# Feed-forward of a Hymba layer on Trainium2: SyncE's transfers in program order, token sums stored eight sums behind, block loads and row stores at steps of their own

## The chip, the cores and the metric

The kernel runs on one core of a Trainium2 chip. The metric is the device time of one execution in microseconds (us). Its runs took 2438.16, 2438.87 and 2443.68 us, a median of 2438.87 us. The execution that the profiler recorded took 2437.08 us, of which 2435.3 us is the span of its trace; 1.8 us lie outside the span. Where a time of the trace is named, it counts from the start of that span.

## The reference

The layer has 2048 tokens of width 1024: two mixers (gated linear attention and dilated sliding-window attention), an output projection, and a feed-forward part with a hidden width of 4096 and a squared ReLU. All of it is computed in float32. The change lies in the feed-forward part alone:

```
h = h + matmul(square(relu(matmul(rmsnorm(h, mlp_norm_g), W_ff1))), W_ff2)
y = rmsnorm(h, final_norm_g)
```

W_ff1 is 1024 x 4096 and W_ff2 is 4096 x 1024.

## The kernel before, in words

Every float32 operand of a matmul is split into a rounded part and the rest of it (`split`: ScalarE writes the rounded part at L414, VectorE the rest at L415), and `mm3` makes three matmuls of 128 x 128 by 128 x 512 of each pair (L134, L135, L136). So each operand passes ScalarE and VectorE before TensorE can use it.

**First matmul of the feed-forward part (FF1 below, 1127 to 1828 us).** The work is cut into 32 blocks g: two halves of the tokens by 16 slices of 256 hidden columns. A block is done in 7 jobs instead of 8, by a scheme of Strassen's kind, in the order 1, 2, 5, 6, 3, 4, 7; a job is 12 matmuls. `prep1` makes the weight operand of a job two jobs ahead: it splits a piece of the block's raw weights, and between the jobs VectorE adds and subtracts pieces of them in place (L1158 after job 1's and 2's split, L1160 to L1163 later). There are two raw buffers, `w1raw`, so the load of block g+2 (`load_w1`, L1143, 1 MB) may be issued only once the split for job 7 of block g is done, and L1158 of block g+2 waits for it. `product1` runs the 12 matmuls and takes the bank out of PSUM; the results of a block are four tiles c11, c12, c21, c22 in `acc1`, to which ScalarE applies ReLU and the square (L1186, L1187). c21 and c22 come last, with job 7 (VectorE L1201 to L1203 ahead of them).

**Token sums.** The second matmul works on sums of hidden blocks. After every two blocks, 14 jobs, `token_sums` is begun: 28 additions on GpSimd (`SUMS`, L1224), on pieces of 128 x 256 in the `acc1` tiles and in three scratch pieces at the end of the tile `xt`. Each entry of `SUMS` is (result, left, sign, right, index of the stored result or None); 0 to 15 are pieces of the two blocks, 16 and above the scratch. SyncE writes 26 results of a pair of blocks to the array `actD` in device memory (L1218): four pieces as they are (`SINGLES`) and those sums that have an index. One pair of blocks is called a period below.

**Second matmul (FF2 below, 1828 us to the end).** 26 products of two halves make 52 phases of 48 matmuls. A phase is 8 steps of 6 matmuls; steps are counted from the start of FF2, and FF1's last jobs have negative steps, two to a job. `load_s` reads a token operand from `actD` into the buffers `rs` (L1282), `prep_s` splits it into `cs` (L1296, L1298, L1300); `load_t` reads a block of weights into `rt` or, for the third buffer, into two `acc1` tiles (L1312); `add_t` adds or subtracts weight blocks on GpSimd (L1320) and stores one result as `tD`; `prep_t` splits into `ct`. `load_c` reads rows of h into `sum` or `acc1` (L1336), `taken` adds the phase's banks to them, and `output` normalizes the rows and stores them (L1355, L1356). Functions are run at the steps given by the tables at the end.

**What sets the order.** On every engine instructions run in the order in which the scheduler of the language has put them. It works from the program's order and its own estimate of durations and may move an instruction ahead of others. SyncE (SP in the profile, SPq for its queue) only issues transfers: one that waits holds up all that stand behind it.

Of the kernel before, what the change touches and what calls it, by code (L numbers as in the profile page):

```python
# [69 lines left out]
SUMS = [  # L70
# [7 lines left out]
]  # L78
# [27 lines left out]
NB = 6  # L106


def emit(tc, a, stop=99):
# [38 lines left out]
    xt = const.tile([128, 1280], F32, name="xt")  # L148
# [1058 lines left out]
    def act_tiles(g):  # L1207

        t = [acc1[(g - g % 2 + k // 2) % 4][:, 1024 * (k % 2) + 256 * m:1024 * (k % 2) + 256 * m + 256]
             for m in range(4) for k in range(4)]  # L1210
        return t + [xt[:, 512 + 256 * i:768 + 256 * i] for i in range(3)]

    def token_sums(g):

        half, c, t = g // NP, g % NP // 2, act_tiles(g)

        def store(r, v):
            SP.dma_start(actD[r, half, :, c], v)  # L1218

        for l, r in SINGLES:  # L1220
            store(r, t[l])
        yield
        for l, x, op, y, r in SUMS:
            G.tensor_tensor(t[l], t[x], t[y], op=OP.add if op == "+" else OP.subtract)  # L1224
            if r is not None:
                store(r, t[l])
            yield
# [56 lines left out]
    def prep_s(ph, u):  # L1284
# [16 lines left out]
        load_s(ph + 2, u)  # L1301
# [12 lines left out]
    def add_t(q, u):  # L1314

        _, _, _, add, stored = WEIGHTS[q]
        if add is not None:
            d, x, op, y = add
            d, x, y = [traw(b, u // 2)[:, u % 2 * 2:u % 2 * 2 + 2] for b in (d, x, y)]
            G.tensor_tensor(d, x, y, op=OP.add if op == "+" else OP.subtract)  # L1320
            if stored:
                SP.dma_start(tD[:, 2 * u:2 * u + 2], d)
# [15 lines left out]
    def output(half, l, i):  # L1338
# [16 lines left out]
        SP.dma_start(out2[row:row + 128, 512:], C[1])  # L1355
        (A if (half, l, i) == (1, 3, 1) else SP).dma_start(out2[row:row + 128, :512], C[0])  # L1356
# [18 lines left out]
    steps = {}  # L1375
# [4 lines left out]
    def step(n):  # L1380
        for f, args in steps.pop(n, ()):
            f(*args)

    for ph in range(2 * NR):
        for u, n in ((0, -7), (1, -3)):
            at_step(4 if (ph, u) == (1, 1) else 8 * ph + n, prep_s, ph, u)
    for q, at in enumerate(first_of):
        at *= 16
        for h, n in ((0, -23), (1, -17)):
# [12 lines left out]
    rb.append(slot("rb"))  # L1402
    back = [*back, reload(order[3], 0), reload(order[4], 0), reload(order[5], 0, slot("rt"))]
    load_w1(1)
    for at in range(7):
        if at == 2:
            norm_to_T(*late)
        if back:
            list(back.pop(0))
        if at == 1:  # L1410
            back.append(reload(order[6], 0))
        prep1(at + 2)
        product1(at)


    first, parts_at = 7 * (NP - 1), {}
    for n in range(14):
        parts_at.setdefault(first + 1 + n * 4 // 5, []).append(n // 2)
    halves, begun = {}, set()
    ts = iter(())  # L1420
    for at in range(7, len(jobs1)):
        if at == first - 2:
            halves.update({n: reload(order[n], 1) for n in range(2)})
        prep1(at + 2)
        product1(at)
        for _ in range(2 if at % 14 else 3):
            next(ts, None)
        if at % 14 == 13:
            ts = token_sums(at // 7)
        for n in parts_at.get(at, ()):  # L1430
            next(halves[n])
            if n in begun and n + 2 < 7:
                halves[n + 2] = reload(order[n + 2], 1)
            begun.add(n)
        for n in range(2):
            step(2 * (at - len(jobs1)) + n)

    P, left = {}, None
    for ph in range(2 * NR):
        if PRODUCTS[ph // 2][1]:  # L1440
            P[ph % 2] = [bank() for _ in range(2)]
        p = P[ph % 2]
        for k in range(8):
            step(8 * ph + k)
            if ph == 0:
                for _ in range(3 if k < 4 else 5):
                    next(ts, None)
            if left and k < 2:
                taken(ph - 1, k, left[k])
            if ph < 2 * NR - 1 or k < 2:  # L1450
                for i in range(2):
                    mm2(p[i], ph, k, i)
        left = p
    for i in range(2):
        for k in range(2, 8):
            mm2(left[i], 2 * NR - 1, k, i)
        taken(2 * NR - 1, i, left[i])
# [55 lines left out]
```

## Time and profile before

| what | value |
|---|---|
| runs, median of 3 | 2438.87 us |
| profiled execution, its own time | 2437.08 us |
| its span | 2435.3 us |
| PE busy | 2292.4 us, 94% of the span |
| DVE busy | 1704.7 us, 70% |
| POOL busy | 1179.3 us, 48% |
| ACT busy | 1166.5 us, 48% |
| mean granted TensorE clock | 0.976 |
| transfers | 430.78 MB, mean 177 GB/s |

PE is TensorE's matmuls, DVE VectorE, ACT ScalarE, POOL GpSimd. An engine's share is a mean over stages that have different limits, so a stage is read from its own rows: how many matmuls it ran, how long they took, and what PE waited for. In a row of waits the columns are the waiting engine, its tile and line, the engine or transfer that released it, and then us in total, how often, and the longest. In a row of the timeline stand the start, the length, engine, line, operation, result and inputs, and in brackets the idle time of the engine before it with what ended it. One execution was recorded; its time stands 1.8 us below the median of the runs.

### The profile page before, as it was taken

Reading aid. Unit: us, or ns where it says so; the run is one execution under the profiler, and the core shown is the slowest. Engines: PE = TensorE matmul, PEld = TensorE weight load, DVE = VectorE, ACT = ScalarE, POOL = GpSimd, SP = SyncE. Lnnn points to the kernel's source line nnn. Section 1 sums busy time; section 2 is a strip of 40 time slices with the busy share of each in tenths; the row PEclk is TensorE's granted clock in tenths of the full one; section 3 lists DMA queues with packets and bytes.
Section 4 is the critical chain, followed back from the end, with each engine's and each line's share of the span. In section 5 each row is a group of like instructions: output and inputs, shape, how many; then the busy total and the mean of one; then the engine's idle time right before and its main releaser. Section 6 shows DMA issues by size and latency. Waiting matters only on the chain. (4 is left out here: it accounts for less than half of the span.)

```text
span 2435.3 us, 35693 instructions
## 1 busy us (share of the span) xinstructions
PE 2292.4 (94%) x12456; PEld 1964.1 (81%) x12456; DVE 1704.7 (70%) x2802; ACT 1166.5 (48%) x2227; POOL 1179.3 (48%) x1098
## 2 busy tenths in 40 slices
PE   6999999999999998999998898899899899999998
PEld 6877998789999996888777776777677688888877
DVE  6888768766667774457666568666676787866896
ACT  5565436435777771234444446444443333333454
POOL 5333324345478684000466466666564752431674
PEclk8999999999999999999999899999999999999999
DMA  6458744767667773677343447443348653534463
GB/s 155 120 167 244 246 148 125 239 191 236 193 215 226 248 245 114 206 258 254 117 128 119 126 132 222 139 130 120 122 128 288 206 200 127 193 119 142 140 233 117
DMA packets 340371, 430.78 MB, mean 177 GB/s; under 512 B 20773, under 2 KB 270134, under 8 KB 333663
## 3 DMA queue, kind: packets, MB, share of 16 engines
q1 hardware_dynamic: 340046, 428.24, 55.4%
q8 instruction: 98, 1.61, 0.3%
q14 instruction: 83, 0.67, 0.1%
q10 hardware_dynamic: 144, 0.26, 0.0%
HBM read 276.60 MB, written 156.54 MB: 178 GB/s over the span
## 5 line engine op out<-in xcount | busy, mean ns | idle before, releaser
L415 DVE TENSOR_TENSOR w1comb<-w1raw,w1comb 128x512 fp32r<-128x512 f32 x224 | 186.9, 838 | 65.3 <-ACT w1comb L414 65.1
L414 ACT ACTIVATE w1comb<-w1raw 128x512 fp32r<-128x512 f32 x224 | 135.5, 624 | 200.8 <-DVE w1raw L1160 179.3
L1296 ACT ACTIVATE cs<-rs 128x1024 fp32r<-128x1024 f32 x104 | 109.2, 1051 | 190.1 <-PE ps_c L136 92.9
L724 ACT ACTIVATE pe<-pe,O 128x256 f32<-128x256 f32 (+1 forms) x384 | 155.8, 454 | 57.8 <-DVE O L723 53.2
L752 PE MATMUL ps_a<-v,pt 128*128 128x65 f32 x1200 | 179.6, 251 | 0.7 <-DVE pt L742 0.7
L752 PEld LDWEIGHTS ps_a<-v,pt 128*128 128x128 f32 x1200 | 175.6, 194 | 2.2 <-DVE pt L742 0.9
L1224 POOL TENSOR_TENSOR xt<-acc,acc 128x256 f32<-128x256 f32 x48 | 45.0, 937 | 259.9 <-ACT acc L1187 207.7
L162 POOL TENSOR_TENSOR stats<-stats,mhalf 128x1 f32<-128x1 f32 (+1 forms) x64 | 46.1, 723 | 247.4 <-DVE stats L161 247.3
L733 PE MATMUL ps_d<-ident,pe 128*128 128x128 f32 x600 | 159.9, 279 | 0.0
L723 DVE CUSTOM_DVE_ANT_0 pe<-ps_c,nb 128x256 f32<-128x256 f32 (+1 forms) x384 | 126.8, 361 | 42.0 <-PE ps_d L733 17.6
L415 DVE TENSOR_TENSOR ct<-rt,ct 128x1024 fp32r<-128x1024 f32 x68 | 121.6, 1794 | 41.2 <-ACT ct L414 41.1
L135 PE MATMUL ps_c<-hb,w1comb 128*128 128x512 f32 x336 | 134.9, 401 | 16.3 <-DVE w1comb L415 16.3
L1186 ACT ACTIVATE acc<-acc 128x512 f32<-128x512 f32 x128 | 80.4, 631 | 142.7 <-DVE acc L1198 59.7
L270 ACT ACTIVATE wcomb<-wraw 128x512 fp32r<-128x512 f32 (+2 forms) x126 | 96.6, 773 | 96.6 <-POOL wraw L276 20.0
L136 PE MATMUL ps_c<-ct,cs 128*128 128x512 f32 x360 | 141.9, 394 | 0.0
L134 PE MATMUL ps_c<-ct,cs 128*128 128x512 f32 x360 | 141.8, 394 | 0.0
L135 PE MATMUL ps_c<-ct,cs 128*128 128x512 f32 x360 | 141.6, 393 | 0.0
L1224 POOL TENSOR_TENSOR acc<-acc,acc 128x256 f32<-128x256 f32 x128 | 139.5, 1094 | 2.4
L134 PE MATMUL ps_c<-hb,w1comb 128*128 128x512 f32 x336 | 133.5, 397 | 1.0 <-ACT w1comb L414 1.0
L1158 DVE TENSOR_TENSOR w1raw<-w1raw 128x512 f32<-128x512 f32 x32 | 22.4, 701 | 159.1 <-DMA w1raw<-w_ff 159.1
L136 PE MATMUL ps_c<-hb,w1comb 128*128 128x512 f32 x336 | 133.1, 396 | 0.0
L1224 POOL TENSOR_TENSOR acc<-acc 128x256 f32<-128x256 f32 x128 | 128.1, 1006 | 3.8
(370 smaller groups left out, 7960.3 us busy)
## 6 DMA issues: line engine op xcount, KB each, us to landing
rs<-actD SPq DMA_DIRECT2D x103, 512.0 KB, 4.6
actD<-acc SPq DMA_DIRECT2D x304, 128.0 KB, 2.0
w1raw<-w_ff SPq DMA_DIRECT2D x32, 1024.0 KB, 6.7
rt<-w_ff SPq DMA_DIRECT2D x24, 1024.0 KB, 6.4
k<-kD SPq DMA_DIRECT2D x16, 1024.0 KB, 8.3
actD<-xt SPq DMA_DIRECT2D x112, 128.0 KB, 1.9
rb<-hTD SPq DMA_DIRECT2D x13, 1024.0 KB, 6.8
wraw<-w_in SPq DMA_DIRECT2D x48, 256.0 KB, 3.6
```

What stands on the lines that cost most here:

```text
L134: T.matmul(out, sh, mh, start=first, stop=False, skip_group_check=more)
L135: T.matmul(out, sl, mh, start=False, stop=False, skip_group_check=more)
L136: T.matmul(out, sh, ml, start=False, stop=last, skip_group_check=more)
L270: A.activation(hi, src, AF.Copy, scale=sc)
L414: A.activation(hi, src, AF.Copy)
L415: V.tensor_tensor(lo, src, hi.bitcast(F32), op=OP.subtract)
L723: V.tensor_tensor_reduce(p, s, bias, scale=1.0, scalar=BIG, op0=OP.add, op1=OP.min, accum_out=nm)
L724: A.activation(p, p, AF.Exp, bias=nm, scale=-1.0)
L733: T.transpose(pb[:, i * 128:i * 128 + 128], src, ident)
L752: T.matmul(self.b.opsum[:, n % 4], self.pt[:, i * 128:i * 128 + 128], self.b.v[:, blk, cols], start=first, stop=last)
L1224: G.tensor_tensor(t[l], t[x], t[y], op=OP.add if op == "+" else OP.subtract)
L1296: A.activation(v[:, 0, cs], x, AF.Copy, scale=float(sign))
```

## The change

SyncE's instructions of the feed-forward part are taken out of the scheduler's hands (`tc.manual_schedule(engines={SP.engine})`): they are issued in the order in which the program writes them. The other engines are scheduled as before. Beside it:

- `SUMS` is a new list of 28 sums that gives the same stored results, with four scratch pieces: two in `xt`, two in the upper half of `gM`. `xt` is 256 elements shorter.
- The store of a sum is written `BEHIND` = 8 sums after it, the stores of `SINGLES` at the third sum. Three sums are written after each job (two before, three after the first job of a period), and those of the last period over the phases 0 to 3 (all in phase 0 before).
- `load_s` leaves `prep_s` and is written at steps of its own, 15 steps ahead of the `prep_s` that uses it; the first `load_t` of a weight block and the first `prep_s` of a phase are one step later.
- Stores of `tD` and of output rows are written 4 steps later, but for those of the last 6 steps.

The body of the feed-forward part is only indented; what else changes in it is shown.

```diff
-    xt = const.tile([128, 1280], F32, name="xt")
+    xt = const.tile([128, 1024], F32, name="xt")
...
-        return t + [xt[:, 512 + 256 * i:768 + 256 * i] for i in range(3)]
+        return t + [v[:, 512 + 256 * i:768 + 256 * i] for v in (xt, gM) for i in range(2)]
...
-        for l, r in SINGLES:
-            store(r, t[l])
-        yield
-        for l, x, op, y, r in SUMS:
-            G.tensor_tensor(t[l], t[x], t[y], op=OP.add if op == "+" else OP.subtract)
-            if r is not None:
-                store(r, t[l])
+        for i in range(len(SUMS) + BEHIND):
+            if i == 2:
+                for l, r in SINGLES:
+                    store(r, t[l])
+            if i >= BEHIND and SUMS[i - BEHIND][4] is not None:
+                store(SUMS[i - BEHIND][4], t[SUMS[i - BEHIND][0]])
+            if i < len(SUMS):
+                l, x, op, y, _ = SUMS[i]
+                G.tensor_tensor(t[l], t[x], t[y], op=OP.add if op == "+" else OP.subtract)
             yield
...
-        load_s(ph + 2, u)
...
-                SP.dma_start(tD[:, 2 * u:2 * u + 2], d)
+                at_step(now[0] + 4, SP.dma_start, tD[:, 2 * u:2 * u + 2], d)
...
-        SP.dma_start(out2[row:row + 128, 512:], C[1])
-        (A if (half, l, i) == (1, 3, 1) else SP).dma_start(out2[row:row + 128, :512], C[0])
+        later(out2[row:row + 128, 512:], C[1])
+        if (half, l, i) == (1, 3, 1):
+            A.dma_start(out2[row:row + 128, :512], C[0])
+        else:
+            later(out2[row:row + 128, :512], C[0])
...
+    def later(*args):
+
+        if now[0] < 16 * NR - 6:
+            at_step(now[0] + 4, SP.dma_start, *args)
+        else:
+            SP.dma_start(*args)
...
-        for u, n in ((0, -7), (1, -3)):
+        for u, n in ((0, -6), (1, -3)):
             at_step(4 if (ph, u) == (1, 1) else 8 * ph + n, prep_s, ph, u)
+            if ph > 1:
+                at_step(max(8 * ph + n - 15, 9 if (ph, u) == (3, 1) else -99), load_s, ph, u)
...
-        for h, n in ((0, -23), (1, -17)):
+        for h, n in ((0, -22), (1, -17)):
...
+    with tc.manual_schedule(engines={SP.engine}):
...
-        for _ in range(2 if at % 14 else 3):
+            for _ in range(3):
...
-            if ph == 0:
-                for _ in range(3 if k < 4 else 5):
+                if ph < 4:
+                    for _ in range(2 - k % 2):
```

The first place is SyncE's queue in a middle period of FF1. Before, this stands ahead of and behind the load of an odd block (`w1raw_11505`); `actD_102<-` is a store of a token sum, "waits Pool_49" a wait for the sum itself, "DMAHW" one for an earlier transfer:

```order
776 L1218 DMA actD_102<-acc1_11520 128x256 [waits DMAHW0_49,Pool_49]
777 L1218 DMA actD_102<-acc1_11520 128x256 [waits DMAHW1_49,Pool_49]
778 L1218 DMA actD_102<-acc1_11520 128x256 [waits DMAHW2_49,Pool_49]
779 L1218 DMA actD_102<-acc1_11520 128x256 [waits DMAHW3_49,Pool_49]
780 L1218 DMA actD_102<-acc1_11519 128x256 [waits DMAHW4_49,Pool_49]
781 L1218 DMA actD_102<-acc1_11520 128x256 [waits DMAHW5_49,Pool_49]
782 L1218 DMA actD_102<-xt_74 128x256 [waits DMAHW6_49,Pool_49]
783 L1143 DMA w1raw_11505<-w_ff1 128x8x256 [waits DMAHW7_49,DVE_49]
784 L1218 DMA actD_102<-acc1_11517 128x256 [waits DMAHW0_49,Pool_49]
```

In the changed kernel the same place on SyncE, with the load of an odd block as `w1raw_11507`:

```order
793 L1219 DMA actD_102<-acc1_11520 128x256 [waits DMAHW1_49,Pool_49]
794 L1219 DMA actD_102<-acc1_11520 128x256 [waits DMAHW2_49,Pool_49]
795 L1219 DMA actD_102<-acc1_11519 128x256 [waits DMAHW3_49]
796 L1219 DMA actD_102<-acc1_11519 128x256 [waits DMAHW4_49]
797 L1219 DMA actD_102<-gs_10008 128x256 [waits DMAHW5_49]
798 L1219 DMA actD_102<-acc1_11519 128x256 [waits DMAHW6_49]
799 L1219 DMA actD_102<-xt_74 128x256 [waits DMAHW7_49]
800 L1219 DMA actD_102<-gs_10008 128x256 [waits DMAHW0_49]
801 L1219 DMA actD_102<-acc1_11519 128x256 [waits DMAHW1_49,Pool_49]
802 L1219 DMA actD_102<-acc1_11520 128x256 [waits DMAHW2_49]
803 L1144 DMA w1raw_11507<-w_ff1 128x8x256 [waits DMAHW3_49,DVE_49]
```

Before, each store ahead of the load waits for its own sum, and the last one, from `xt`, stores a sum of the next period. Now row 794 stores the sum that GpSimd makes as the 27th of the period's 28, row 801 waits for the 28th, and the others in between were made before these; three stores of the period stand behind the load.

The second place is GpSimd at the begin of the last period, which runs into FF2. Before (`xt_74` is the scratch, the `acc1` tiles are the two blocks):

```order
886 L1224 TENSOR_TENSOR xt_74<-acc1_11519,acc1_11520 128x256 [waits Activation_49]
887 L1224 TENSOR_TENSOR acc1_11519<-acc1_11520 128x256 [waits Pool_49]
888 L1224 TENSOR_TENSOR acc1_11520<-acc1_11520 128x256 [waits DMAHW0_49,Pool_49]
889 L1224 TENSOR_TENSOR xt_74<-acc1_11520 128x256 [waits DMAHW6_49]
890 L1224 TENSOR_TENSOR xt_74<-acc1_11519,xt_74 128x256 [waits DMAHW4_49,Pool_49]
```

The same place in the changed kernel (`gs_10008` holds the two new scratch pieces, the blocks' tiles have other numbers):

```order
885 L1229 TENSOR_TENSOR xt_74<-acc1_11521,acc1_11522 128x256 [waits DMAHW6_49,Activation_49]
886 L1229 TENSOR_TENSOR gs_10008<-acc1_11521,xt_74 128x256 [waits DMAHW1_49,Pool_49]
887 L1229 TENSOR_TENSOR acc1_11522<-acc1_11521,acc1_11522 128x256
888 L1229 TENSOR_TENSOR acc1_11522<-acc1_11522 128x256
889 L1229 TENSOR_TENSOR acc1_11521<-acc1_11521 128x256 [waits Pool_49]
890 L1229 TENSOR_TENSOR gs_10008<-gs_10008 128x256 [waits Pool_49]
891 L1229 TENSOR_TENSOR acc1_11521<-acc1_11521 128x256 [waits Pool_49]
892 L1229 TENSOR_TENSOR acc1_11521<-acc1_11522,acc1_11521 128x256 [waits Pool_49]
893 L1229 TENSOR_TENSOR acc1_11522<-acc1_11522 128x256 [waits DMAHW3_49]
```

Before, row 889 overwrites a scratch piece that an early sum of the same period left there to be stored, so it waits for that store; now the pieces written in the first rows are those of the period before, and the first piece that is overwritten behind a store of the same period comes at row 893.

The third place is ScalarE where FF2 begins. Before (`ct` is a weight operand made of the raw weights `rt`, `cs` a token operand made of `rs`, or of `acc1` for the last piece of phase 1):

```order
1579 L1187 ACTIVATE acc1_11520<-acc1_11520 128x512 [waits Activation_49] x2
1580 L414 ACTIVATE ct_16599<-rt_16502 128x1024 [waits DMAHW1_49,PE_49]
1581 L1296 ACTIVATE cs_16449<-rs_16306 128x768 [waits DMAHW2_49,PE_49]
1582 L414 ACTIVATE ct_16661<-rt_16502 128x1024
1583 L1296 ACTIVATE cs_16449<-acc1_11520 128x256 [waits PE_49,Activation_49]
```

The same place in the changed kernel:

```order
1576 L1188 ACTIVATE acc1_11522<-acc1_11522 128x512 [waits Activation_49] x2
1577 L1299 ACTIVATE cs_16483<-rs_16311 128x768 [waits DMAHW5_49,PE_49]
1578 L1299 ACTIVATE cs_16483<-acc1_11522 128x256 [waits PE_49,Activation_49]
1579 L415 ACTIVATE ct_16587<-rt_16508 128x1024 [waits DMAHW6_49]
1580 L415 ACTIVATE ct_16627<-rt_16508 128x1024
```

The two pieces of the token operand of phase 1 stood behind the weight operand `ct`; now they stand ahead of it. VectorE's instructions for the same tiles are moved in the same way. In the rest of FF1, VectorE, ScalarE and TensorE keep their order.

More of the change, by code (lines that the diff above doesn't have):

```diff
@@ L106 @@
 NB = 6
+BEHIND = 8
 def emit(tc, a, stop=99):
@@ L1373, in mm2 @@
             PRODUCTS[ph // 2][1] == 1 and c == 0, c == 7, PRODUCTS[ph // 2][1] == 0)
-    steps = {}
+    steps, now = {}, [0]
+    def later(*args):
[3 more added lines that the diff above has]
+            SP.dma_start(*args)
     def at_step(n, f, *args):
@@ L1380, in step @@
     def step(n):
+        now[0] = n
         for f, args in steps.pop(n, ()):
@@ L1400, in emit @@
             at_step(4 * ph + u - 20, load_s, ph, u)
[L1402 to L1425, printed above, removed]
-        for _ in range(2 if at % 14 else 3):
[L1427 to L1444, printed above, removed]
-            if ph == 0:
-                for _ in range(3 if k < 4 else 5):
[L1447 to L1453, printed above, removed]
```

54 lines of the change are left out of this document (50 added, 4 removed), and 14 rows, old and new, of the table SUMS.

## The prediction

> **What bounds the kernel now.** I read the table by stretches first, because the mean over the span hides where PE idles. Its columns are the stretch, its length, busy time and instructions of PE, PEld, DVE, ACT and POOL, the granted clock, the DMA share and GB/s.
>
> ```profile
> 1127.00:1828.00 701.00, 636.77 (x2679) 514.87 (x2678) 465.47 (x595) 340.38 (x593) 406.75 (x415) 0.96 0.44 139
> 1828.00:1900.00 72.00, 66.74 (x282) 53.93 (x281) 46.53 (x54) 22.42 (x27) 34.69 (x35) 0.95 0.79 279
> 1900.00:2000.00 100.00, 90.53 (x374) 73.16 (x373) 82.06 (x48) 34.66 (x34) 66.69 (x23) 0.95 0.63 204
> 2000.00:2300.00 300.00, 300.00 (x1325) 248.64 (x1324) 230.47 (x195) 116.08 (x124) 111.39 (x41) 1.00 0.43 143
> 2300.00:2400.00 100.00, 97.57 (x423) 79.97 (x421) 92.10 (x83) 51.28 (x80) 74.67 (x36) 0.98 0.59 199
> ```
>
> From 2000 to 2300 us PE never idles at a clock of 1.00: 300/1325 = 0.2264 us a matmul. At that pace FF1's 2679 matmuls are 606.5 us, so FF1 loses 701 - 606.5 = 94.5 us. FF2 loses 72 - 63.8 = 8.2 us to 1900, 100 - 84.7 = 15.3 us to 2000, and 100 - 95.8 = 4.2 us after 2300. The stages before 1127 us aren't touched. So 94.5 us in FF1 and 23.5 us at FF2's begin are what the change can win; in the 300 us between it can only lose.
>
> Who is waited for, from the waits of PE in FF1, then of DVE and of POOL from 1127 to 1900 us:
>
> ```profile
> PE ps_a L135 <- DVE w1comb L415: 27.5, 9, 4.7
> ...
> DVE w1raw L1158 <- DMA w1raw<-w_ff: 155.0, 28, 9.8
> ...
> POOL xt L1224 <- DMA actD<-xt: 82.7, 23, 26.5
> ```
>
> In FF1 PE waits for weight splits, and DVE, which makes them, for the load of the raw block at L1158. One period of FF1 from the timeline, engine by engine, shows why that load is late:
>
> ```profile
> 1702.87 0.39 SPq L1143 DMA_DIRECT2D w1raw<-w_ff  x1
> 1720.75 0.38 SPq L1143 DMA_DIRECT2D w1raw<-w_ff  x1
> 1746.72 0.32 SPq L1218 DMA_DIRECT2D actD<-acc  x1
> 1747.13 0.40 SPq L1143 DMA_DIRECT2D w1raw<-w_ff  x1
> ...
> 1709.52 0.69 DVE L1158 TENSOR_TENSOR w1raw<-w1raw 128x512 f32<-128x512 f32 x1 [9.20 <-DMA w1raw<-w_ff]
> 1739.62 0.77 DVE L415 TENSOR_TENSOR w1comb<-w1raw,w1comb 128x512 fp32r<-128x512 f32 x1 [1.77 <-ACT w1comb L414]
> ...
> 1710.87 0.79 PE L135 MATMUL ps_a<-hb,w1comb 128*128 128x512 f32 x1 [4.11 <-DVE w1comb L415]
> ...
> 1714.99 0.62 ACT L1187 ACTIVATE acc<-acc 128x512 f32<-128x512 f32 x1
> 1716.03 0.62 ACT L1187 ACTIVATE acc<-acc 128x512 f32<-128x512 f32 x1
> ...
> 1716.73 0.74 POOL L1224 TENSOR_TENSOR xt<-acc,acc 128x256 f32<-128x256 f32 x1 [13.60 <-ACT acc L1187]
> 1728.40 0.77 POOL L1224 TENSOR_TENSOR xt<-acc,acc 128x256 f32<-128x256 f32 x1 [2.89 <-DMA actD<-xt]
> 1738.41 0.74 POOL L1224 TENSOR_TENSOR xt<-acc 128x256 f32<-128x256 f32 x1
> 1743.99 1.19 POOL L1224 TENSOR_TENSOR acc<-acc 128x256 f32<-128x256 f32 x1
> 1745.14 0.74 POOL L1224 TENSOR_TENSOR xt<-acc 128x256 f32<-128x256 f32 x1
> 1745.95 1.43 POOL L1224 TENSOR_TENSOR acc<-acc 128x256 f32<-128x256 f32 x2
> ```
>
> The load at 1747.13 overwrites a buffer whose last reader, job 7's split, ended at 1739.62 + 0.77 = 1740.39. It comes 6.7 us later because SP first issued the store at 1746.72, which waited for a sum. Then a loop closes. The load lands, L1158 starts 6.65 us after its issue (1702.87 to 1709.52), and behind it on DVE stands the taking out of job 7's bank, then ACT's squares, then the first sum that needs them, 13.86 us after the load's issue (1716.73). From there to 1745.14 run 25 sums with one wait of 2.89: (28.41 - 2.89)/25 = 1.02 us a sum. Two sums more and the store make 1.58, the next load 0.41: 13.86 + 28.41 + 1.58 + 0.41 = 44.26 us a period, what the two loads stand apart. The 14 jobs of a period would take PE 168 x 0.2264 = 38.0 us. The difference of 6.2 us, times some 14 periods, is 87 of FF1's 94.5 us: GpSimd's sums and SP's order bound FF1, not PE. PE sees it as a wait of 4.11 and a first matmul of 0.79 behind it.
>
> **The change in FF1.** DVE, ACT and PE keep their order there, so what remains is the loop.
> - Its start: the run of sums that the load hangs on now begins with one that needs the square of c21, not of c22. The two squares stand 1716.03 - 1714.99 = 1.04 us apart: 13.86 - 1.04 = 12.82.
> - The sums: the load stands behind the 27th sum's store, and one of the 28 runs ahead of c21, so 26 sums lie between. With four scratch pieces and stores that are written eight sums later, no sum waits for a store of its own period: the 2.89 goes. At 1.02 each, 26.5.
> - The stores: nine now stand in a row between the 27th sum and the load, at the 0.41 from the store at 1746.72 to the load at 1747.13: 3.7. That is what replaces one store.
> - Sum: 12.82 + 26.5 + 3.7 = 43.0, against 44.26: -1.2. Against it go two costs that the trace doesn't show. Nine stores just ahead may delay the load's landing; a store takes 2.0 us to land, which bounds it by 0 and some 1.7 (2.0 less the issue's 0.3), and as the stores are issued 0.41 apart, so that most are done, I take 0.3. And the sums closer together may meet DVE more often: 0.74 where DVE waits (the sum at 1738.41 before DVE's start at 1739.62), 1.19 where it works (1743.99). For the three sums that fill the gap of 2.89 that is 0 to 3 x 0.45 = 1.3; taken 0.3, since the mean of 1.02 has the mixture in it.
>
> ```profile
> actD<-acc SPq DMA_DIRECT2D x304, 128.0 KB, 2.0
> ```
>
> So -0.6 a period, times 14: **-8 us**, with bounds of -1.2 (neither cost) and +1.8 (both in full) a period: -17 to +25.
>
> The nine stores are where a rule of the Trainium skill speaks against the change. In "DMA: Bandwidth & Descriptors", Queues, rings and completion order, it says that each DMA engine works off descriptors in the order of their ring, and SP has one ring on each; so a load can't pass the stores ahead of it. With the page's limit of 358 GB/s from HBM per core, taken for the stores too, nine of 128 KB would be an estimate of 3.3 us; they take SP 3.7 to issue, so hardly any would be left when the load comes. No run here shows it yet.
>
> The other loads, of even blocks, are on time now (1720.75) and have three fewer stores of old sums ahead of them; zero. The shorter scratch and the added list entries cost nothing.
>
> **The change at FF2's begin.** The last period's sums and what hung on them:
>
> ```profile
> 1873.12 0.74 POOL L1224 TENSOR_TENSOR xt<-acc 128x256 f32<-128x256 f32 x1 [26.46 <-DMA actD<-xt]
> 1896.49 0.74 POOL L1224 TENSOR_TENSOR acc<-acc 128x256 f32<-128x256 f32 x1
> 1905.34 4.70 POOL L1320 TENSOR_TENSOR rt<-acc,rt 128x1024 f32<-128x1024 f32 x2 [8.11 <-DMA acc<-w_ff]
> ...
> 1898.45 1.72 SPq L1312 DMA_DIRECT2D acc<-w_ff  x2
> ...
> 1853.59 1.06 ACT L414 ACTIVATE ct<-rt 128x1024 fp32r<-128x1024 f32 x1 [9.36 <-DMA rt<-w_ff]
> 1855.43 0.80 PE L134 MATMUL ps_d<-ct,cs 128*128 128x512 f32 x1 [4.25 <-ACT cs L1296]
> ```
>
> The fourth sum stood 26.46 us for a scratch piece that was still to be stored. So the sums ended at 1897, the `acc1` tiles came free for weights at 1898, and the first add of weights began at 1905.34, late for FF2's third weight block: the 15.3 us. With four pieces the first wait for a store of the same period comes at the eleventh sum. It is for one of the four pieces stored as they are. If DMA's backlog (279 GB/s to 1900 us) keeps that until 1858, the 18 sums left take 13 to 18 us at 0.74 to 1.02, and the end lies near 1874. Adding up to 6 us for later waits, the weight loads come at about 1880 and the adds at 1887, 18 us earlier. That is more than PE lost here, so the cause goes; what comes next are loads of 1 MB of the same kind, for which I leave 4 of the 15.3: **-11** (0 to -15).
>
> The 8.2 us to 1900: ACT's 9.36 us for `rt` held up the `cs` pieces behind it in its order, for which PE waited 4.25. They now stand ahead of `ct`. The next that is late is `ct` itself, whose load lands as before at 1853.6, some steps ahead of its use. I take half of what the 4.25 and the slow matmuls behind it cost: **-3** (+2 to -7).
>
> In the steady stretch each `load_s` is issued a step after the split that frees its buffer, 15 steps of 6 x 0.2264 = 1.36 us ahead of its use, 20 us, against 4.6 us to land (below); zero. Stores of `tD` and rows go out 4 steps, 5.4 us, later on SP. Behind them stand loads with leads over ten steps; if that cover were gone, one landing of 6.4 us each time. The rows of the last six steps aren't moved, so the tail is as before. One step on `load_t` and `prep_s` is 1.36 us of 20 to 30; zero.
>
> ```profile
> rs<-actD SPq DMA_DIRECT2D x103, 512.0 KB, 4.6
> rt<-w_ff SPq DMA_DIRECT2D x24, 1024.0 KB, 6.4
> ```
>
> SP in program order means that a load may stand behind a store whose sum isn't made, without a scheduler to pass it. I leave 0 to +8 for that in FF2 and take 0.
>
> **The sum.** 2437.1 of the profiled execution - 8 - 11 - 3 = 2415; it stands 1.8 below the median of the runs, so **2417 us** for those. The own range of this case, FF1 at -16 to +2 and FF2 at -18 to -6: 2405 to 2435.
>
> **The rivals.**
> - *Sums become quick.* If they run near 0.85, without waits and with DVE idle less in their way, a period is 12.8 + 26 x 0.85 + 3.7 = 38.6, nearly PE's 38.0: 14 x 5.7 = 80 us from FF1, with FF2 2345 us. A mean of 0.93 gives 14 x 3.6 = 50: about 2375. For it: 0.74 rows stand in the trace. Against: DVE's order and work in that window stay. Chance 0.14.
> - *It moves little.* SP's burst takes back what the gap gave (0 in FF1), and a next wait takes FF2's (half of 14): 2432, and to 2446 with +1 a period. Chance 0.17.
> - *Slower: the load behind the burst.* The period is 16.5 + 26d with d the mean of a sum, and is longer than 44.26 from d = 1.068. If the sums meet DVE throughout, at 1.1, and the load lands 0.9 later behind the nine stores, it is 46.0: 14 x 1.75 = +25, less 10 in FF2: 2453 us. For it: rows of 1.19 are many, and the load has nine stores between itself and the 27th of 28 sums. Against: the wait of 2.89 goes for sure. "GPSIMD Engine Reference", Specifications, in the Trainium skill says the same of the mechanism: GpSimd shares its SBUF interfaces with VectorE and contends with VectorE instructions that have two SBUF inputs, as L415 is; the rows of 0.74 and 1.19 agree. Chance 0.14.
>
> That the order isn't carried out isn't a case: SP's new order is in the program.
>
> **How the numbers follow.** My forecast has 0.55. A measurement of this kernel can tell 0.3%, 7.3 us, from no change: to 2431.6 is faster. Nine tenths of my case and all of the quick one lie there, and a little of the third: 0.69 faster. Same: most of the third, 0.17. Slower: 0.14. The range leaves out most of the quick case (under 2382) and most of the slower one (over 2446): 2382 to 2446, 0.8 inside.
>
> **What would show it.** Right: odd loads 43 to 44 us apart with nine stores 0.41 apart ahead of each; no wait of POOL for `actD<-xt` in FF1; weight loads into `acc1` by 1882 and no PE wait around 1910 to 1940. Wrong: POOL's mean in FF1 off 1.02, odd loads that don't wait for the stores, a period bound by something else than load to squares to sums to load, or waits of PE from 2000 to 2300 us.

## The result, and the profile after

The changed kernel took 2425.48 us (median of 6 runs, 2420.76 to 2429.61) against 2441.17 us of the kernel before in the same and the earlier runs (median of 6, 2435.78 to 2447.05): a ratio of 0.9934 with a 95% interval of 0.9915 to 0.9954. It is faster by 16 us, where 22 were forecast. Its profiled execution has a span of 2423.6 us, 11.7 less than that of before; the stages below are read from these two executions.

The same stretches as before, with the same columns; FF2 begins some 8 us earlier, so the first row ends at 1820:

```profile
1127.00:1820.00 693.00, 633.67 (x2664) 508.81 (x2662) 470.19 (x592) 337.17 (x588) 423.09 (x421) 0.97 0.44 138
1820.00:1900.00 80.00, 79.70 (x342) 65.57 (x343) 58.32 (x62) 29.98 (x37) 38.26 (x35) 0.97 0.94 332
1900.00:2000.00 100.00, 94.47 (x407) 77.02 (x406) 71.77 (x54) 36.12 (x36) 43.46 (x15) 0.98 0.51 170
2000.00:2300.00 300.00, 297.17 (x1303) 245.23 (x1302) 233.73 (x194) 117.19 (x129) 129.66 (x49) 0.99 0.45 148
2300.00:2400.00 100.00, 93.66 (x400) 76.45 (x399) 85.96 (x82) 48.18 (x77) 63.16 (x32) 0.97 0.53 178
```

At 0.2264 us a matmul FF1 still loses 693 - 603 = 90 us. FF2 loses 2.6 us to 1900 and 7.9 to 2000, where it lost 8.2 and 15.3. But from 2000 to 2300 us it now loses 300 - 295 = 5 us, where it lost none, and after 2300 9.4 in place of 4.2.

PE runs the same 12456 matmuls in nearly the same order in both kernels, so the start of the n-th one can be set side by side. Each place below is such a start; the last column is what was won (-) or lost since the row above:

| place | before, us | after, us | after - before | since the row above |
|---|---|---|---|---|
| FF1's begin | 1129.47 | 1126.56 | -2.9 | -2.9 |
| FF1, after 8 periods | 1482.19 | 1467.38 | -14.8 | -11.9 |
| after 10 periods | 1567.00 | 1557.61 | -9.4 | +5.4 |
| after 15 periods | 1789.32 | 1776.84 | -12.5 | -3.1 |
| after 16 periods, FF2's begin | 1834.70 | 1827.54 | -7.2 | +5.3 |
| FF2, phase 8 | 1944.73 | 1916.39 | -28.3 | -21.2 |
| phase 12 | 1988.25 | 1966.40 | -21.9 | +6.5 |
| phase 38 | 2271.13 | 2249.97 | -21.2 | +0.7 |
| phase 46 | 2362.83 | 2341.37 | -21.5 | -0.3 |
| phase 50 | 2406.35 | 2394.68 | -11.7 | +9.8 |
| last matmul | 2427.88 | 2416.21 | -11.7 | 0.0 |

The first row isn't the change's: nothing of it runs there, and among the executions below this place lies between 1126.1 and 1135.9 us. So in these two executions the change gave 4.3 us in FF1 and 4.5 in FF2, 8.8 together, and both are differences of larger parts. From phase 38 to 46 the sum hides a trade: phase 39 now loses 4.4 us, and the 4.6 that phase 44 lost before are gone. What the later phases lose on balance, 9.8 us, they lose in the phases 46, 47 and 49.

**FF1.** SyncE, DVE and POOL in one period of the changed kernel:

```profile
1643.47 0.44 SPq L1219 DMA_DIRECT2D actD<-acc  x1
1643.95 0.45 SPq L1219 DMA_DIRECT2D actD<-xt  x1
1644.44 0.45 SPq L1219 DMA_DIRECT2D actD<-gs  x1
1644.99 0.88 SPq L1219 DMA_DIRECT2D actD<-acc  x2
1645.97 0.39 SPq L1144 DMA_DIRECT2D w1raw<-w_ff  x1
...
1690.05 0.39 SPq L1144 DMA_DIRECT2D w1raw<-w_ff  x1
...
1652.61 0.69 DVE L1159 TENSOR_TENSOR w1raw<-w1raw 128x512 f32<-128x512 f32 x1 [7.86 <-DMA w1raw<-w_ff]
...
1658.78 0.74 POOL L1229 TENSOR_TENSOR xt<-acc 128x256 f32<-128x256 f32 x1 [11.37 <-ACT acc L1188]
...
1682.92 3.09 POOL L1229 TENSOR_TENSOR acc<-acc 128x256 f32<-128x256 f32 x3
1690.90 0.74 POOL L1229 TENSOR_TENSOR gs<-acc 128x256 f32<-128x256 f32 x1 [4.89 <-DMA actD<-gs]
```

The odd load still stands behind a row of stores, DVE still waits 7.86 us for it, and the sums run from 1658.78 to 1686.01 without a wait between them: 27 in 27.23 us. The wait of 2.89 is gone as forecast. The wait of 4.89 at 1690.90 costs nothing, since the sums behind it wait for ACT's squares anyway.

**FF2's begin.** The last period's sums, the weight loads into `acc1` and the first add of weights:

```profile
1849.94 1.06 POOL L1229 TENSOR_TENSOR acc<-acc 128x256 f32<-128x256 f32 x1 [9.95 <-DMA actD<-acc]
1864.85 1.72 POOL L1229 TENSOR_TENSOR acc<-acc 128x256 f32<-128x256 f32 x1
1880.49 4.76 POOL L1322 TENSOR_TENSOR rt<-acc,rt 128x1024 f32<-128x1024 f32 x2 [13.92 <-DMA acc<-w_ff]
...
1874.29 0.38 SPq L1314 DMA_DIRECT2D acc<-w_ff  x1
```

The wait of 26.46 has become one of 9.95, the sums end 31 us earlier (1866.6 for 1897.2, where 1874 was forecast), and the adds begin 24.9 us earlier.

**New waits.** First, at the end of FF1, on ACT, PE and SyncE:

```profile
1816.26 2.00 ACT L415 ACTIVATE ct<-rt 128x1024 fp32r<-128x1024 f32 x2 [7.29 <-DMA rt<-w_ff]
1818.17 0.61 ACT L415 ACTIVATE w1comb<-w1raw 128x512 fp32r<-128x512 f32 x1
...
1818.83 0.80 PE L135 MATMUL ps_c<-hb,w1comb 128*128 128x512 f32 x1 [5.51 <-ACT w1comb L415]
...
1809.18 0.32 SPq L1219 DMA_DIRECT2D actD<-xt  x1
1809.55 1.05 SPq L1314 DMA_DIRECT2D rt<-w_ff  x2
```

FF2's first weight load goes out right behind a store that waited for its sum; ACT waits 7.29 us for it, and a weight split of FF1's last jobs stands behind that on ACT. In the kernel before, these two loads had gone out at 1501.56 and 1512.41 us, some 310 us ahead of their split. Second, ahead of phase 39 of FF2, from the transfer to PE:

```profile
2231.08 0.43 SPq L1314 DMA_DIRECT2D acc<-w_ff  x1
2238.90 3.67 SPq L1285 DMA_DIRECT2D rs<-actD  x2
2242.62 0.43 SPq L1314 DMA_DIRECT2D rt<-w_ff  x1
...
2250.43 4.75 POOL L1322 TENSOR_TENSOR acc<-rt,acc 128x1024 f32<-128x1024 f32 x2 [5.93 <-DMA rt<-w_ff]
...
2252.86 1.06 ACT L415 ACTIVATE ct<-acc 128x1024 fp32r<-128x1024 f32 x1 [6.28 <-POOL acc L1322]
...
2253.95 2.31 DVE L416 TENSOR_TENSOR ct<-acc,ct 128x1024 fp32r<-128x1024 f32 x1 [4.96 <-ACT ct L415]
...
2263.67 0.50 PE L136 MATMUL ps_d<-ct,cs 128*128 128x512 f32 x1 [2.43 <-DVE cs L1301]
```

Between two weight loads (2231.08 and 2242.62) SyncE issues only two token loads, and for most of these 11.1 us it stands waiting to issue them. The second weight load lands at 2250.3: the add waits 5.93 us for it, ACT 6.28 for the add, DVE 4.96 for ACT, and the token split behind it on DVE comes too late for PE. Third, ahead of phase 47; this phase and the one before lose 8.3 us:

```profile
2334.05 4.75 SPq L1395 DMA_DIRECT2D out<-sum  x4
...
2339.39 0.41 SPq L1314 DMA_DIRECT2D rt<-w_ff  x1
...
2347.48 4.74 POOL L1322 TENSOR_TENSOR rt<-rt 128x1024 f32<-128x1024 f32 x2 [3.80 <-DMA rt<-w_ff]
...
2349.90 1.06 ACT L415 ACTIVATE ct<-rt 128x1024 fp32r<-128x1024 f32 x1 [7.05 <-POOL rt L1322]
...
2358.03 0.80 PE L136 MATMUL ps_d<-ct,cs 128*128 128x512 f32 x1 [3.21 <-DVE cs L1303]
```

From the weight load (2339.39) to PE the chain is the same, but what stands ahead of the load is different: four stores of output rows, which wait for VectorE to scale the rows (the third until 2338). Over 400 us, from phase 14 to 50, SyncE waits 20.1 us for VectorE in such stores; in the scheduler's order below it waits 5.1 us in the same phases.

### The profile page after: what moved, and what is told of

Same layout as the page of the kernel before. It is cut to its first block, busy times and chain, and to the rows that moved or that the text cites. A ratio compares the mean times of both kernels' runs of the same rounds, so it can differ in the third digit from the quotient of the medians.

```text
span 2423.6 us, 35461 instructions
## 1 busy us (share of the span) xinstructions
PE 2288.7 (94%) x12456; PEld 1956.2 (81%) x12456; DVE 1702.2 (70%) x2802; ACT 1165.8 (48%) x2227; POOL 1182.6 (49%) x1098
## 4 chain that ended last, share of the span: by engine, by line
PE 48%; POOL 17%; issue 14%; DVE 10%; DMA 8%; ACT 2%; SPq 2%; POOLq 0%; DVEq 0%; ACTq 0%
POOL acc L1229 8%; PE ps_a L136 5%; PE ps_a L137 5%; PE ps_a L135 5%; PE ps_a L753 4%; POOL gs L1229 3%; PE ps_c L136 3%; PE ps_c L137 3%; PE ps_c L135 3%; PE ps_d L734 3%; DMA rt<-w_ff 2%; PE ps_c L712 2%; PE ps_c L714 2%; DVE ct L416 2%; POOL xt L1229 2%
## 5 line engine op out<-in xcount | busy, mean ns | idle before, releaser
L1229 POOL TENSOR_TENSOR acc<-acc 128x256 f32<-128x256 f32 x160 | 168.5, 1066 | 15.5 <-DMA actD<-acc 15.4
L136 PE MATMUL ps_c<-hb,w1comb 128*128 128x512 f32 x336 | 134.3, 400 | 11.7 <-DVE w1comb L416 11.7
L415 ACT ACTIVATE ct<-rt 128x1024 fp32r<-128x1024 f32 x68 | 71.5, 1059 | 132.8 <-POOL rt L1322 79.5
L273 DVE TENSOR_TENSOR wcomb<-wraw,wcomb 128x512 fp32r<-128x512 f32 (+2 forms) x84 | 100.5, 1200 | 38.0 <-ACT wcomb L271 37.6
L1159 DVE TENSOR_TENSOR w1raw<-w1raw 128x512 f32<-128x512 f32 x32 | 26.2, 819 | 138.3 <-DMA w1raw<-w_ff 137.2
```

What stands on the lines that cost most here:

```text
L136: T.matmul(out, sl, mh, start=False, stop=False, skip_group_check=more)
L273: V.tensor_tensor(lo, src, hi.bitcast(F32), op=OP.subtract)
L415: A.activation(hi, src, AF.Copy)
```

## The experiments

The theory after the result (A): SyncE's place in the order is what counts. In FF1 the odd block's load stands behind stores that wait for the last sums, which closes the loop of the prediction; in FF2 weight loads stand behind token loads that wait (the stores of output rows above are not in it). The rivals: the distance of eight did it (B1), the engines' own chains bound a period and the load waits for something else (B2), or the program's order helps by itself (B3).

The table has the median of each run's executions and its ratio to the runs of the kernel before on the same chip. The last three columns are from the profiled execution of each: FF1 from its begin to its 16th period, FF2 to phase 12, and the rest, by the starts of the same matmuls as above. One caution for all rows: where SyncE's order changes, the scheduler also places some instructions of the other engines anew, so a run doesn't change SyncE alone. From phase 12 on, for example, some 40 of ScalarE's 225 instructions and as many of GpSimd's 87 stand elsewhere in the changed kernel than in the one with the scheduler's order.

| kernel | us | ratio, 95% interval | FF1 | to phase 12 | rest |
|---|---|---|---|---|---|
| before | - | 1 | 705.2 | 153.6 | 439.6 |
| changed | 2425.48 | 0.9934 [0.9915, 0.9954] | 701.0 | 138.9 | 449.8 |
| scheduler's order on SyncE | 2376.86 | 0.9744 [0.9718, 0.9771] | 647.2 | 149.2 | 439.8 |
| stores one sum behind | 2425.15 | 0.9945 [0.9923, 0.9967] | 693.7 | 144.1 | 449.4 |
| odd load ahead of the stores | 2368.68 | 0.9705 [0.9686, 0.9725] | 636.2 | 138.5 | 450.8 |
| weight loads 5 steps earlier | 2435.49 | 0.9980 [0.9967, 0.9993] | 698.0 | 141.4 | 453.3 |
| odd load ahead, scheduler from phase 12 | 2359.79 | 0.9663 [0.9647, 0.9678] | 639.2 | 138.2 | 439.7 |
| odd load ahead, token loads 5 steps later | 2363.25 | 0.9668 [0.9651, 0.9684] | 637.4 | 137.2 | 445.1 |
| two orders, first weight load earlier | 2355.39 | 0.9644 [0.9624, 0.9663] | 631.4 | 149.8 | 441.7 |
| before with the new list alone | 2382.78 | 0.9763 [0.9739, 0.9786] | 650.0 | 150.2 | 439.8 |
| before with the program's order alone | 2450.90 | 1.0048 [1.0032, 1.0063] | 695.5 | 156.9 | 457.7 |

**The scheduler's order again.** One line of the changed kernel:

```diff
-    with tc.manual_schedule(engines={SP.engine}):
+    if True:
```

> All of the change, but SyncE's order left to the scheduler again. Theory A (the odd block's load stands behind the period's last stores on SyncE, and the program's order gives back in FF2 what it wins): the odd load stays behind the stores of the last sums, so a period stays within 1 us of 43.5 and FF1 within 10 us of the changed kernel; in FF2 the phases 38 to 50 lose under 4 us instead of 14. Time 2415 to 2430 us. Rival B (the program's order itself is what made FF1 shorter, and the new list of sums did nothing): a period back at 44.3 or more, the first phases of FF2 lose their 23 us again, time 2435 to 2445 us.

Measured 2376.86 us: far quicker than either theory said. FF1 is 54 us shorter than in the changed kernel, not within 10. The end of theory A holds nearly (439.8 us from phase 12 on, as before; the phases 38 to 50 lose 4.9 us where under 4 were expected), and FF2's begin is 10 us longer than in the changed kernel. SyncE in one period of FF1:

```profile
1610.43 0.38 SPq L1144 DMA_DIRECT2D w1raw<-w_ff  x1
...
1628.92 0.32 SPq L1219 DMA_DIRECT2D actD<-gs  x1
1629.34 0.38 SPq L1144 DMA_DIRECT2D w1raw<-w_ff  x1
...
1650.00 0.38 SPq L1144 DMA_DIRECT2D w1raw<-w_ff  x1
```

A period takes 1650.00 - 1610.43 = 39.6 us. The scheduler, given the new list, puts each load behind stores of sums that are ready; only one load of a period is late, by some 2 us. So the step "the odd load stays behind the last stores" was wrong for this order, while its reason, that the load's place in the queue sets the period, is borne out.

**The stores one sum behind**, in the program's order:

```diff
-BEHIND = 8
+BEHIND = 1
```

> The stores are written one sum behind instead of eight, in the program's order. Theory A: SyncE then waits for each sum as it is made, and the load of an even block, on time now, stands behind the stores of sums that GpSimd makes 11 to 14 sums into the period: it is issued some 7 us late, as the odd one is, and costs PE about 4 us more a period. 14 periods: +40 to +70 us, 2465 to 2495 us. Rival B (the distance of eight does nothing, since GpSimd's order sets when a sum is ready): within 7 us of the changed kernel.

Measured 2425.15 us, as the changed kernel: the expectation of theory A is missed by 40 us or more. Loads and their readers in FF1:

```profile
1631.19 0.39 SPq L1144 DMA_DIRECT2D w1raw<-w_ff  x1
1643.08 0.38 SPq L1144 DMA_DIRECT2D w1raw<-w_ff  x1
1673.84 0.39 SPq L1144 DMA_DIRECT2D w1raw<-w_ff  x1
1685.97 0.38 SPq L1144 DMA_DIRECT2D w1raw<-w_ff  x1
...
1637.85 0.69 DVE L1159 TENSOR_TENSOR w1raw<-w1raw 128x512 f32<-128x512 f32 x1 [6.55 <-DMA w1raw<-w_ff]
1649.08 0.69 DVE L1159 TENSOR_TENSOR w1raw<-w1raw 128x512 f32<-128x512 f32 x1 [2.83 <-DMA w1raw<-w_ff]
```

The load of the even block is indeed late now, DVE waits 6.55 us for it, but the odd one behind it is on time (2.83). A period is 1673.84 - 1631.19 = 42.65 us. The loop has only moved to the other load; I had added the two where one takes the other's place. That the time of the expectation's rival B came out doesn't say that the distance does nothing: to phase 12 FF2 takes 5 us longer here.

**The odd load ahead of the stores.** The ten stores from the 16th sum on are held until the load is out; SyncE stays in program order:

```diff
+        held = []
         for i in range(len(SUMS) + BEHIND):
...
-                store(SUMS[i - BEHIND][4], t[SUMS[i - BEHIND][0]])
+                held.append((SUMS[i - BEHIND][4], t[SUMS[i - BEHIND][0]]))
+            if not 23 <= i <= 32 or g == 2 * NP - 1:
+                for s in held:
+                    store(*s)
+                held = []
```

> The ten stores that stand between the even block's part of a period and the odd block's load are written behind that load; nothing else is changed. Theory A (the load stands behind the stores, and these behind the sums, is what bounds FF1): the odd load is issued within 0.5 us of job 7's split, DVE waits about 2.5 us for it instead of 8, a period comes to between 38 and 40 us, FF1 50 to 75 us shorter, time 2350 to 2375 us. Rival B (the chain of split, matmuls, squares and sums on the engines bounds a period, and the load would only wait for something else, such as a free buffer): a period still above 43 us and the time within 7 us of the changed kernel. Rival C (the held stores keep scratch pieces occupied): GpSimd waits for stores at the begin of a period and half of the gain is lost, 2380 to 2400 us.

Measured 2368.68 us, as theory A said; B2 is out. SyncE, and DVE's wait for the odd load at 1638.29:

```profile
1618.03 0.40 SPq L1144 DMA_DIRECT2D w1raw<-w_ff  x1
...
1638.29 0.38 SPq L1144 DMA_DIRECT2D w1raw<-w_ff  x1
1638.89 1.51 SPq L1219 DMA_DIRECT2D actD<-acc  x3
...
1656.63 0.39 SPq L1144 DMA_DIRECT2D w1raw<-w_ff  x1
...
1644.73 0.69 DVE L1159 TENSOR_TENSOR w1raw<-w1raw 128x512 f32<-128x512 f32 x1 [2.73 <-DMA w1raw<-w_ff]
...
1647.69 0.84 POOL L1234 TENSOR_TENSOR gs<-acc 128x256 f32<-128x256 f32 x1 [7.63 <-DMA actD<-gs]
1651.44 0.74 POOL L1234 TENSOR_TENSOR xt<-acc 128x256 f32<-128x256 f32 x1 [2.90 <-ACT acc L1188]
```

DVE waits 2.73 us in place of 7.86, a period is 1656.63 - 1618.03 = 38.6 us, and PE's 168 matmuls take 38.0. POOL does wait for a held store (7.63), but then still 2.90 for ACT: rival C has its wait and not its cost.

**The weight loads 5 steps earlier.** With this a load of `tD` is written ahead of its stores, so it reads what was there earlier:

```diff
-        for h, n in ((0, -22), (1, -17)):
+        for h, n in ((0, -27), (1, -22)):
```

> In FF2 the loads of weight blocks are written 5 steps earlier (27 and 22 ahead instead of 22 and 17), so that each stands ahead of one pair of token loads that it stood behind. Theory A (the new waits of FF2 come from weight loads that stand on SyncE behind token loads which wait for a split): the waits of PE at the phases 8 to 12, 38 to 40 and 46 to 50, 20 us in the changed kernel, fall to under 8; time 2408 to 2418 us. Rival B (the loads are late because their buffers come free late, or DVE has too much to do there): the same waits, the token loads now late as well, time 2422 to 2435 us.

Measured 2435.49 us, 10 slower than the changed kernel and just above rival B's range. In the profiled execution FF2 is 6 us longer than in the changed kernel (2.5 to phase 12, 3.5 behind it) and FF1 3 shorter; the other 7 us of the medians it doesn't place. The place of these loads alone doesn't cure the waits: SyncE spends 323 us of some 400 in token loads that wait (167.3 and 155.4), here as in the changed kernel (182.3 and 143.2), and a weight load that is moved past one or two of them stands behind the next. But the amount of this waiting isn't the loss: in the scheduler's order it is 246 us too (137.0 and 109.1), with 4.9 us lost by PE. SyncE's waits in this run:

```profile
SPq L1285 <- DVE cs L1303: 167.3, 37, 10.2
SPq L1285 <- DVE cs L1301: 155.4, 26, 12.7
```

**Two orders.** The odd load ahead, and from phase 12 on SyncE is the scheduler's again:

```diff
+            if ph == 12:
+                by_hand.close()
```

> As the run with the odd load ahead of the stores (2368.7 us), and SyncE's order is left to the scheduler from phase 12 of FF2 on. Theory A (the program's order gives back some 14 us after phase 38, since loads stand behind token loads that wait): FF1 and FF2 to phase 12 as in that run, the waits of the phases 38 to 50, 8 us there, gone but for 2; time 2358 to 2364 us. Rival B (those waits belong to the engines' orders, which the change set as well): within 4 us of 2368.7.

Measured 2359.79 us; its interval lies below that of the run with the odd load ahead alone. From phase 12 on it takes 439.7 us, the time of before, where that run took 450.8. PE's waits there, in full:

```profile
PE ps_a L136 <- DVE cs L1308: 2.5, 2, 2.0
```

So the new waits of the later phases go when SyncE's order is given back. That they don't belong to the engines' orders, rival B, isn't shown: with SyncE's order the other engines got theirs back as well. From phase 12 on ScalarE's rows have the sequence of before, and VectorE's and GpSimd's differ from it in one or two places. The chains above, from a late load to PE, speak for SyncE; no run separates the two.

**The token loads 5 steps later**, with the odd load ahead and the program's order throughout:

```diff
-                at_step(max(8 * ph + n - 15, 9 if (ph, u) == (3, 1) else -99), load_s, ph, u)
+                at_step(max(8 * ph + n - 10, 9 if (ph, u) == (3, 1) else -99), load_s, ph, u)
```

> As the run with the odd load ahead of the stores (2368.7 us), with all of FF2 in the program's order, but the token loads are written 10 steps ahead of their use instead of 15. Theory A (weight loads are late because token loads that cannot be issued yet stand ahead of them): SyncE waits less for token splits (324 us from phase 14 to 50 there, under 200 here), the waits of PE after phase 38 gone but for 2, time 2358 to 2364 us. Rival B (the token loads become late instead: 10 steps are 13.6 us, a load takes 4.6 us to land): new waits of PE for cs over all phases, 2375 us or more.

Measured 2363.25 us, in theory A's range, and the rest of FF2 takes 445.1 us: half of the loss is back. The condition was not met, though: SyncE still waits 284 us (171.4 and 112.9) for token splits where under 200 were expected. PE's waits after phase 38 didn't go but for 2 us either: they are 5.9 us, and phase 47 still takes 6.4 us longer than an undisturbed one, behind row stores in which SyncE now waits 38.9 us. So writing the token loads later helps, and it doesn't reach the loads that stand behind row stores.

**The first weight load earlier**, with the two orders:

```diff
-            at_step(max(at + n, -4 + 3 * h) if q else -18 + h, load_t, q, h)
+            at_step(max(at + n, -4 + 3 * h) if q else -26 + h, load_t, q, h)
```

> As the kernel with two orders in this batch, and the first weight load of FF2 is written 8 steps (4 jobs) earlier. Theory A (at FF1's end ScalarE's split of the first weight block waits 7 us for its load, which stands on SyncE behind a store, and holds up two weight splits of FF1 behind it): PE's waits of 4.1 and 3.2 us there go, and the matmuls run at the full clock behind them; 5 to 9 us less than the kernel with two orders. Rival B (the buffer of that load isn't free earlier, or its landing is slowed by what else is loaded there): within 3 us of it.

Measured 2355.39 us, 4 under the kernel with two orders, but the intervals overlap (0.9624 to 0.9663 and 0.9647 to 0.9678): not told apart. FF1 is 7.8 us shorter in the profiled execution, as theory A said, and FF2 to phase 12 is 11.6 longer there; that execution was the slowest of the kernel's four (2363.34), so whether the gain is given back each time is open.

**Two parts of the change alone, in the kernel before.** The new list with the fourth piece; here one piece of phase 1's token operand is taken after a sum has overwritten it:

```diff
-SUMS = [(16, 9, '+', 11, 16), (16, 6, '+', 7, 18), ...]
+SUMS = [(16, 9, '+', 11, 16), (17, 6, '+', 7, 18), ...]
-        return t + [xt[:, 512 + 256 * i:768 + 256 * i] for i in range(3)]
+        return t + [v[:, 512 + 256 * i:768 + 256 * i] for v in (xt, gM) for i in range(2)]
```

> The kernel before with one part of the change alone: the new list of sums and the fourth scratch piece; each store is written right behind its sum and SyncE's order is the scheduler's. Theory A (it is the list with four pieces that lets the odd load stand further ahead on SyncE, as in the run with the scheduler's order): FF1 as there, a period of 40 to 41 us, FF2's begin as before, 2372 to 2385 us. Rival B (the distance of eight or the steps of FF2 made that run quick): within 7 us of the kernel before.

And SyncE in program order with the old list:

```diff
+    with tc.manual_schedule(engines={SP.engine}):
```

> The kernel before with another part alone: SyncE's transfers of the feed-forward part in program order, stores right behind their sums, the old list and three pieces. Theory A (the program's order is what costs, by loads that stand behind waiting stores and token loads): not faster than before, 2440 to 2475 us, with both loads of a period late or one late by over 6 us, and new waits of PE in FF2 after 2000 us. Rival B (the order helps by itself, 10 us or more, by taking the last stores of FF1 out of the way of FF2): 2415 to 2432 us.

Measured 2382.78 and 2450.90 us, both in theory A's range; B1 and B3 are out. The list alone wins 2.4%, as much as the whole change does in the scheduler's order (the intervals overlap), the order alone loses 0.5%, and in the change they don't add: together they win 0.7%. FF1 shows it: 705.2 before, 650.0 with the list, 695.5 with the order, 701.0 with both.

## Why the prediction was right, and where it was not

The time lies in the range, and the sign and the loop were right. Part of it is luck: the range of 2382 to 2446 us held the kernel before, too, and the steps below give 8.8 us in the two profiled executions, where the sum had 22; errors of both signs cancel in them. Of the signs that the prediction named, the odd loads came 43 to 44 us apart and the weight loads for `acc1` by 1876; but PE waits at 1910 to 1940 us (2.2 and 1.4), where it was to have no wait, and from 2000 to 2300 us (2.4 and 0.4), which was named as a sign of being wrong. By its steps:

- *The loop of FF1* (load, split, bank, squares, sums, store, load): shown by the run that takes the load out of it, 65 us less in FF1. The start of 12.82 measured 1658.78 - 1645.97 = 12.81, the sum's 1.02 measured 27.23/27 = 1.01. From 1602.59 to 1777.01 lie four periods between odd loads, 43.6 us each; 43.0 + 0.6 was forecast.

```profile
1602.59 0.40 SPq L1144 DMA_DIRECT2D w1raw<-w_ff  x1
...
1777.01 0.40 SPq L1144 DMA_DIRECT2D w1raw<-w_ff  x1
```

- *The nine stores* are the one term of it that was small: 43.6 - 12.8 - 26.2 = 4.6 us for 3.7, since they go out 0.37 to 0.55 apart, 0.48 in the mean, not 0.41, and one of the four bursts has a pause of 1.4. The extra cost that I kept for the load's landing didn't come: 1652.61 - 1645.97 = 6.64 for 6.65 before.
- *FF1, -8.* Measured -4.3. Thirteen periods won 15.0 us, nearly twice the 8 that were forecast for fourteen, and two places that the sum left out took 10.7 back. In the ninth and tenth period, behind the loads of the second half's token operands, 5.4 us were lost; why wasn't tried. And the last period took 5.3 us more, with ACT's wait of 7.29 us for FF2's first weight load. On ACT the first split of that block stood ahead of a weight split of FF1 before as well (1819.93 and 1822.39); what is new is the load, which went out at 1809.55 in place of 1501.56. The prediction looked at what the program's order does to the loads in a middle period and not to this one. With the load written 8 steps earlier, in the kernel with two orders, FF1 is 7.8 us shorter.
- *FF2's begin, -14.* Measured -21.2 to phase 8 and +6.5 to phase 12: -14.7. The size is right, and the cause given for it is right only in part. The long wait of the last sums for a store is cut (26.46 to 9.95), but it is cut with the list alone (10.99) and in the scheduler's order (14.66), too. The sums end 44 and 45 us after FF2's begin there, for 39 in the changed kernel and 63 before, and yet FF2's begin is only 3.4 and 4.4 us shorter. The other 10 us need SyncE's program order on top of the new list; alone that order makes FF2's begin 3.3 us longer (156.9). Which of its transfers does it wasn't tried.
- *The steady stretch, 0.* This is the step that failed, in two sentences of the prediction. "Each `load_s` is issued a step after the split that frees its buffer": that it is written there doesn't mean that SyncE gets there early; it stands in a token load that can't go yet for most of the time, and weight loads behind it are late. "Behind them stand loads with leads over ten steps", of the stores of output rows: that cover was gone ahead of phase 47, and the price that the prediction named for this case, one landing of 6.4 us, is about what phase 47 lost (17.09 - 10.88 = 6.2). In all it cost 0.7 - 0.3 + 9.8 = 10.2 us, a little more than the +8 that I had left and then not taken. The run with two orders takes it back (450.8 to 439.7), with the other engines' orders.
- *The rivals.* "Sums become quick" had the right price for a period near PE's 38 us, but the wrong cause: the sums needn't be quicker, the load only has to stand ahead of their stores. The slower one didn't come, since d stayed at 1.01. The rule of the Trainium skill on the order of a ring ("DMA: Bandwidth & Descriptors", Queues, rings and completion order) decided nothing here: the time is lost ahead of the issue, on SyncE, while the landing took as long in these periods with nine stores ahead as with one. The section also lets a later descriptor finish its write first, so the prediction's "can't pass" said more than it does.

What the prediction never asked is what the new list would do without the program's order. The rows of the order gave a reason to ask: in the kernel before, the odd load stood behind a store of the next period, so it was the scheduler that had put it so late, and a new list could move it.

## What to carry to other kernels

On an in-order queue that serves loads and stores, a load's time is set by the slowest thing written ahead of it: look at what each store in front of it waits for, and write a load that the bottleneck waits for ahead of stores that nobody waits for. When a change has a list and an order in it, cost each alone; here the list alone wins 57 us, and with the order and the other parts of the change 16 are left. An order written out by hand can be worth keeping in one stage (FF2's begin, 10 us) and not in the next.

## What the runs showed of the hardware

A sum of 128 x 256 on POOL took 0.73 to 0.74 us where DVE idled and 1.07 to 1.24 where it worked, and DVE's operations are often longer in such stretches as well. In the changed kernel, while POOL runs sums of 1.2 and then none:

```profile
1676.95 1.22 DVE L416 TENSOR_TENSOR w1comb<-w1raw,w1comb 128x512 fp32r<-128x512 f32 x1
1687.27 0.68 DVE L416 TENSOR_TENSOR w1comb<-w1raw,w1comb 128x512 fp32r<-128x512 f32 x1
```

The same split takes 1.22 us beside a sum and 0.68 behind the last one, which ends at 1686.01. It isn't so each time: the split at 1680.99 took 0.68 beside a sum, too. I had costed the sums by it and not DVE's half of it.
